# Modulation vectors of a two-layer hybrid backbone: matrix products on TensorE against weighted sums on VectorE, ScalarE and accumulating DMAs

## The chip, the cores and the metric

One NeuronCore of a Trainium2 chip runs the whole program. The metric is the device time of one execution in microseconds (us), as a median of several runs. Beside it stands one profiled execution, whose rows are quoted here: PE is TensorE, PEld its weight loads, DVE VectorE, ACT ScalarE, POOL GpSimd, SP SyncE. A "q" behind an engine's name means its sequencer, which issues transfers and waits.

## The reference

Two layers work on 512 latent and 256 context tokens of width 1024. A layer first forms modulation vectors from the two conditioning vectors `c` (for the latents) and `c_ctx` (for the context):

```python
mod_x = silu_c @ ada_w[layer] + ada_b[layer]      # [6 * 1024]
mod_c = silu_cc @ ada_w[layer] + ada_b[layer]
sh1, sc1, g1, sh2, sc2, g2 = split(mod_x, 6)      # the same for mod_c
hx = modulate(rmsnorm(x, norm1_g[layer]), sh1, sc1)
mx, mc = hybrid_mixer(hx, hc, w_in[layer], ...)   # retention and gated linear attention
x = x + g1 * (mx @ w_out[layer])
x = x + g2 * squared_relu_mlp(modulate(rmsnorm(x, norm2_g[layer]), sh2, sc2), ...)
```

`ada_w[layer]` is 1024 x 6144 float32, 24 MB for each layer. The first third (`sh1`, `sc1`) is needed before the first projection, `g1` at the output projection, `sh2`, `sc2` at the second norm, `g2` at the end of the MLP.

## The kernel before

Activations lie feature-major, 128 features by tokens. Each large product is made of three products of float32r parts (L437 to L439), so that TensorE carries nearly the whole time. The order of the work is written out by hand: `plan` is a list of items that `run` (L400) emits one after the other, and each engine executes what it was given in that order. Weights arrive as slabs of 128 x 1024 float32 (512 KB) through a ring of four `wraw` tiles; `split` (L241) casts a slab to its high part on ScalarE (L244) and subtracts on VectorE for the low part (L245). Slabs are split up to four ahead of their use, with six split slabs kept.

The attention of a layer follows `SCHEDULE` (L109): one line, here called a row and counted from 0, is one block of projections, 8 to 11 us on TensorE, and after it the stages of heads that run behind it. Stages are short: a few small products of TensorE, and chains of VectorE and ScalarE instructions. In the text, `gB` is VectorE's prefix sum of gates, `gC` ScalarE's exponentials, `qk` VectorE's products of queries and keys, `N` a head's norm.

The modulation vectors of the first layer come in two parts. The first third is made at the start, in quarters (L374, untouched). The remaining two thirds go through `ada_next` (L306): behind the block of each of the rows 0 to 15, `ada_step` loads two 512 KB pieces a step ahead and multiplies one k tile by `cs` with four products of 512 columns (L287, eight records of the profile). The second layer's vectors are made during the first layer's MLP by `ada_sums` (L324), a generator of 54 steps, one behind each MLP item: for each of six units of 1024 columns, eight steps in which VectorE adds weighted pieces to two sums (L340, L342; one for each conditioning vector), and a ninth step in which eight products of 256 columns (L348) with `onehot` add the partitions. The ninth step starts `ada_finish` (L259): ScalarE copies the row, TensorE transposes it, VectorE adds the bias.

The sums of both vectors lie in a tile that shares its place with the tables `rtab`. GpSimd squares in the MLP (L1210), multiplies in the retention stages (L983, L946), and issues a few transfers (reload L1165, spill L1250).

Of the kernel before, what the change touches and what calls it, by code (L numbers as in the profile page):

```python
# [39 lines left out]
class Item:  # L40
    """A piece of the program: emits instructions; may need weight slabs; a stage runs one block after its deps."""
# [5 lines left out]
class Chains:  # L47
    """Instruction chains that hop between engines: each tick emits the next step of every chain under way.

    Queued chains start one per tick, with at most WIDTH of them under way."""  # L50
# [45 lines left out]
class Act:  # L96
    """A moving operand in two float32r parts, made by chains for token ranges."""
# [10 lines left out]
# one block of projections and the attention stages that run behind it, per line; at most NSLOT tiles live  # L108
# [30 lines left out]
def build(ctx: ExitStack, tc, a):  # L139
# [7 lines left out]
    tp = ctx.enter_context(tc.tile_pool(name="tab", bufs=1))  # L147
    mp = ctx.enter_context(tc.tile_pool(name="mp", bufs=NSLOT))
# [23 lines left out]
    def bc(col, n):  # L172
        """[P, c] -> [P, c, n], each value repeated n times."""
        return col.rearrange("p (c o) -> p c o", o=1).to_broadcast([col.shape[0], col.shape[1], n])

    def rep(tab, c):
        """[P, n] -> [P, c, n], the row repeated c times."""
        return tab.rearrange("p (o t) -> p o t", o=1).to_broadcast([tab.shape[0], c, tab.shape[1]])
# [5 lines left out]
    # ---- constants and inputs  # L184
# [32 lines left out]
    # silu(c) of both vectors, as 32 stationary columns (30 of them zero) per k tile  # L217
# [14 lines left out]
    # ---- weight slabs: [128, 1024] and its exact split into two float32r parts  # L232
# [14 lines left out]
    class RankSlab(Slab):  # L247
        """Four copies of 32 columns per k tile: the second one's low part, the others' high parts."""
# [7 lines left out]
    # ---- adaLN vectors: mod[l][p, v, j] for feature 128 j + p  # L256
    mod = [const.tile([P, 2, 48], F32, name=f"mod{l}") for l in range(DEPTH)]

    def ada_finish(l, pt, tiles, n, fold=1):  # L259
        """pt: row 32 c + v holds, for vector v, n features from the tile tiles[c] on; `fold` such parts are summed."""  # L260
# [18 lines left out]
    def ada_step(state, l, g, kk):  # L279
        if kk == 0:  # L280
            state["pt"] = psa.tile([P, 512], F32, tag="psa", name=f"ada_{l}_{g}")
        pt = state["pt"]
        w = state.pop("w", None)
        if w is None:
            w = ada_load(l, g, kk)
        for c in range(4):
            nc.tensor.matmul(  # L287
                pt[32 * c : 32 * c + 32, :], cs[:, kk, :], w[c // 2][:, (c % 2) * 512 : (c % 2 + 1) * 512],
                start=(kk == 0), stop=(kk == KK - 1),
            )  # L290
        if kk == KK - 1:
            state["end", l, g] = ch.start(ada_finish(l, pt, [16 * g + 4 * c for c in range(4)], 512))

    def ada_load(l, g, kk):
        ws = []
        for i in range(2):
            w = wraw.tile([P, WCOL], F32, tag="raw", name=f"adaw_{l}_{g}_{kk}_{i}")
            c0 = g * 2048 + i * WCOL
            nc.sync.dma_start(w, a["ada_w"][l, kk * P : (kk + 1) * P, c0 : c0 + WCOL])
            ws.append(w)  # L300
        return ws

    ada_state = {}
    ada_queue = [(l, g, kk) for l, g in ((0, 1), (0, 2)) for kk in range(KK)]

    def ada_next():  # L306
        if ada_queue:
            l, g, kk = ada_queue.pop(0)
            ada_step(ada_state, l, g, kk)
            if ada_queue:  # L310
                ada_state["w"] = ada_load(*ada_queue[0])

    def ada_drain(l, g):
        while any(q[:2] == (l, g) for q in ada_queue):
            ada_next()
        ch.finish(ada_state["end", l, g])

    # the second layer's: weighted sums over the k tiles on the vector engine, one product to add the partitions
# [5 lines left out]
    def ada_sums(l):  # L324
        acc = tp.tile([P, 2, WCOL], F32, tag="rtab", name=f"adaacc_{l}")
        todo = [(u, kk) for u in range(6) for kk in range(KK)]
# [8 lines left out]
        for i, (u, kk) in enumerate(todo):  # L335
            w, nxt = nxt, load(i + 1) if i + 1 < len(todo) else None
            for v in range(2):
                c = cs[:, kk, v : v + 1]
                if kk == 0:
                    nc.vector.tensor_scalar(acc[:, v], w, c, None, op0=ALU.mult)  # L340
                else:
                    nc.vector.scalar_tensor_tensor(acc[:, v], w, c, acc[:, v], op0=ALU.mult, op1=ALU.add)  # L342
            yield
            if kk == KK - 1:
                pt = psa.tile([P, 512], F32, tag="psa", name=f"ada_{l}_{u}")
                for v in range(2):
                    for c in range(4):
                        nc.tensor.matmul(  # L348
                            pt[32 * c : 32 * c + 32, 0:256], onehot[:, v], acc[:, v, 256 * c : 256 * c + 256],
                            start=(v == 0), stop=(v == 1),  # L350
                        )
                ada_state["end", l] = ch.start(ada_finish(l, pt, [8 * u + 2 * c for c in range(4)], 256))
                yield

    # the first layer's shift and scale, in four quarters of 256 features each
# [18 lines left out]
    def quarter(q, middle=None, end=None):  # L374
        """Shift and scale of a quarter, even and odd k tiles apart."""
# [65 lines left out]
    def project(pt, slab, c0, acts, t0, t1, ks=None, first=0, last=None):  # L441
        """pt[:, :t1 - t0] += W[:, tile].T @ act over the k tiles `ks` of a slab part [kk, 128]."""
# [14 lines left out]
    # ---- RMSNorm over features, for a group of tokens at a time  # L457
    class Norm:
# [3 lines left out]
        def square(self, kk, t0, t1, first):  # L462
            """A chain that adds a tile's squares to the sum."""
# [14 lines left out]
        def late_square(self, kk, t0, t1):  # L478
            """A tile's squares that the product over the partitions adds to the sum."""
# [43 lines left out]
        def apply_all(self, l, shift, v, t0, t1, ks=range(KK)):  # L523
            """Chains that make the tiles `ks` of a group of tokens."""
# [15 lines left out]
    # ---- first norm, and the accumulators of the first three projections  # L540
# [63 lines left out]
    # masks and decay tables  # L604
# [6 lines left out]
    # decay of a key to its chunk's end (forward) or start (backward), per partition  # L611
    kdec = const.tile([P, nrd], F32, name="kdec")

    def setup():
# [5 lines left out]
        # log(1 - exp(ret_decay)) as log1p: ln(u) * e / (1 - u), u = 1 - e rounded  # L620
# [24 lines left out]
    def layer(l, norm):  # L645
        """The layer's items, and the norm that follows it."""
# [10 lines left out]
        def start():  # L657
# [6 lines left out]
            # retention tables per head: in-chunk weights of both directions, query decays  # L664
# [34 lines left out]
        # ---- gate ranks: low parts of the weights in rows 32 to 63, high ones elsewhere; summed by the next product  # L699
# [7 lines left out]
        # ---- gated linear attention's queries and keys, each on both partition halves  # L707
# [27 lines left out]
        def tok_blocks(nm, j0, vt, center):  # L735
            """Values token-major, one tile [token, chunk, 128] per head."""
# [36 lines left out]
        def head_out(idx, po, t0, t1, sq, o):  # L773
            """Evacuate a head's output and its square."""
# [16 lines left out]
        def gla(h):  # L791
# [16 lines left out]
            def gB():  # L808
                # 16 log gate; prefix sums per chunk, from the chunk's middle; backward ones exclusive
# [222 lines left out]
        # ---- output gates and the mixer's output  # L1032
# [47 lines left out]
        # ---- the first three projections' items  # L1080
# [354 lines left out]
```

## Time and profile before

| | us |
|---|---|
| median of 3 runs (lowest to highest) | 1659.46 (1658.64 to 1659.53) |
| the profiled execution, first to last instruction | 1658.9 |
| PE busy | 1618.7 (98%) |
| DVE busy | 946.9 (57%) |
| ACT busy | 629.5 (38%) |
| POOL busy | 201.6 (12%) |
| mean granted TensorE clock | 0.992 of full |

Busy time is a share of the whole span; a stage's limit is read from the chain of waits and from the timeline of that stage. In a timeline row the columns are start, duration, engine, line, operation, output and inputs, shapes, count, and in brackets the idle time before it with what ended it; matmuls overlap, so what one costs is read from the distance of starts.

### The profile page before, as it was taken

To read this page: it belongs to the slowest core of one execution; us is meant where nothing else is said; L and a number is where in the kernel's file an instruction comes from. 1 tells how busy PE (TensorE), PEld (TensorE's weight loads), DVE (VectorE), ACT (ScalarE), POOL (GpSimd) and SP (SyncE) were. 2 spreads that over 40 slices of the span, in tenths; PEclk is the share of its full clock that TensorE was granted. 3 is DMA by queue.
4 is the path that set the end of the run, shared out by engine and by line. 5 is a ranking of instruction groups with operands and counts; after the bars stand their busy time and mean duration, and the time that the engine had idled before them with its cause. 6 is when DMAs were issued, how large, how long until landed. Compare 5 with 4: busy or idle time off the path is not lost. (4 is left out here: it accounts for less than half of the span.)

```text
span 1658.9 us, 22890 instructions
## 1 busy us (share of the span) xinstructions
PE 1618.7 (98%) x9236; PEld 1384.2 (83%) x9236; DVE 946.9 (57%) x1491; ACT 629.5 (38%) x1083; POOL 201.6 (12%) x215
## 2 busy tenths in 40 slices
PE   5999999999999999999999999999999899999997
PEld 3778888888998888888888887888889888888887
DVE  5676664554755555555556476588466633443445
ACT  5535424562532222222212246363464532222232
POOL 3200021110111010110101121001110211010010
PEclk9999999999999999999999999999999999999999
DMA  9533433122323333333333222121123323223321
GB/s 323 175 127 126 137 108 102 39 88 90 103 89 127 115 127 109 120 102 116 126 115 127 95 88 66 51 77 52 51 89 128 103 89 102 91 100 102 102 64 51
DMA packets 57610, 173.80 MB, mean 105 GB/s; under 512 B 6208, under 2 KB 17792, under 8 KB 57504
## 3 DMA queue, kind: packets, MB, share of 16 engines
q1 hardware_dynamic: 55232, 164.85, 30.2%
q0 software_dynamic: 2272, 7.50, 1.2%
q8 instruction: 72, 1.18, 0.3%
q14 instruction: 34, 0.28, 0.0%
HBM read 168.13 MB, written 4.19 MB: 104 GB/s over the span
## 5 line engine op out<-in xcount | busy, mean ns | idle before, releaser
L437 PE MATMUL pm<-yh,hi_m 128*128 128x512 f32 (+1 forms) x800 | 279.6, 349 | 0.0
L437 PE MATMUL pm<-hidh,hi_m 128*128 128x512 f32 (+1 forms) x800 | 279.1, 349 | 0.0
L438 PE MATMUL pm<-yl,hi_m 128*128 128x512 f32 (+1 forms) x800 | 278.6, 348 | 0.0
L438 PE MATMUL pm<-hidl,hi_m 128*128 128x512 f32 (+1 forms) x800 | 278.4, 348 | 0.0
L439 PE MATMUL pm<-yh,lo_m 128*128 128x512 f32 (+1 forms) x800 | 278.2, 348 | 0.0
L439 PE MATMUL pm<-hidh,lo_m 128*128 128x512 f32 (+1 forms) x800 | 277.2, 347 | 0.0
L1208 ACT ACTIVATE relu<-pm 128x512 f32<-128x512 f32 (+1 forms) x100 | 51.1, 511 | 497.6 <-PE pm L439 493.9
L1212 DVE TENSOR_TENSOR hidl<-relu,hidh 128x512 fp32r<-128x512 f32 (+1 forms) x100 | 60.5, 607 | 296.0 <-POOL relu L1210 296.0
L1210 POOL TENSOR_TENSOR relu<-relu 128x512 f32<-128x512 f32 (+1 forms) x100 | 89.2, 893 | 760.3 <-ACT hidh L1209 760.2
L535 DVE SCALAR_TENSOR_TENSOR x<-pm,mod,x 128x512 f32<-128x512 f32 (+1 forms) x200 | 117.6, 640 | 106.6 <-PE pm L439 106.6
L437 PEld LDWEIGHTS pm<-yh,hi_m 128*128 128x128 f32 x800 | 152.6, 191 | 20.2 <-issue 1.2
L437 PEld LDWEIGHTS pm<-hidh,hi_m 128*128 128x128 f32 x800 | 151.5, 189 | 21.3 <-issue 1.1
L438 PEld LDWEIGHTS pm<-yl,hi_m 128*128 128x128 f32 x800 | 152.5, 191 | 18.8
L439 PEld LDWEIGHTS pm<-yh,lo_m 128*128 128x128 f32 x800 | 152.4, 191 | 19.0
L439 PEld LDWEIGHTS pm<-hidh,lo_m 128*128 128x128 f32 x800 | 151.1, 189 | 19.6
L438 PEld LDWEIGHTS pm<-hidl,hi_m 128*128 128x128 f32 x800 | 151.4, 189 | 18.9 <-issue 0.2
L245 DVE TENSOR_TENSOR lo_m<-raw_m,hi_m 128x1024 fp32r<-128x1024 f32 x126 | 154.0, 1222 | 10.6 <-ACT hi_m L244 10.6
L244 ACT CAST hi_m<-raw_m 128x1024 fp32r<-128x1024 f32 x128 | 129.6, 1040 | 51.6 <-DMA raw_m<-in_w_mlp 31.0
L342 DVE SCALAR_TENSOR_TENSOR adaacc<-adaw,cs,adaacc 128x1024 f32<-128x1024 f32 x84 | 103.9, 1278 | 0.0
L245 DVE TENSOR_TENSOR lo_wi<-raw_wi,hi_wi 128x1024 fp32r<-128x1024 f32 x49 | 60.6, 1249 | 29.8 <-ACT hi_wi L244 29.8
L437 PE MATMUL pwo<-yh,hi_wo 128*128 128x256 f32 (+1 forms) x224 | 70.9, 316 | 0.1
L438 PE MATMUL pwo<-yl,hi_wo 128*128 128x256 f32 (+1 forms) x224 | 70.3, 314 | 0.3 <-DVE yl L1056 0.3
(304 smaller groups left out, 2951.5 us busy)
## 6 DMA issues: line engine op xcount, KB each, us to landing
raw_m<-in_w_mlp SPq DMA_DIRECT2D x128, 512.0 KB, 3.5
adaw<-in_ada_w SPq DMA_DIRECT2D x80, 512.0 KB, 3.9
raw_wi<-in_w_in SPq DMA_DIRECT2D x58, 512.0 KB, 4.3
adaw<-in_ada_w SPq DMA_DIRECT2D x32, 256.0 KB, 6.3
raw_wo<-in_w_out SPq DMA_DIRECT2D x16, 512.0 KB, 3.4
x<-in_xT POOLq DMA_DIRECT2D x8, 384.0 KB, 7.8
x<-in_xT SPq DMA_DIRECT2D x8, 256.0 KB, 4.9
raw_wob<-in_w_out SPq DMA_DIRECT2D x4, 512.0 KB, 4.3
```

Of the source, the lines that this page charges most:

```text
L244: nc.scalar.copy(self.hi, self.raw)
L245: self.engine.tensor_sub(self.lo, self.raw, f32(self.hi))
L342: nc.vector.scalar_tensor_tensor(acc[:, v], w, c, acc[:, v], op0=ALU.mult, op1=ALU.add)
L437: nc.tensor.matmul(out, wh, xh, start=first, stop=False)
L438: nc.tensor.matmul(out, wh, xl, start=False, stop=False)
L439: nc.tensor.matmul(out, wl, xh, start=False, stop=last)
L535: nc.vector.scalar_tensor_tensor(xs[kk][:, t0:t1], pt[:, 0 : t1 - t0], mod[l][:, v, gate + kk : gate + kk + 1], xs[kk][:, t0:t1], op0=ALU. ...
L1208: nc.scalar.activation(r, pt[:, 0 : t1 - t0], AF.Relu)
L1210: nc.gpsimd.tensor_mul(r, r, r)
L1212: nc.vector.tensor_sub(a_.lo[:, t0:t1], r, f32(a_.hi[:, t0:t1]))
```

## The change

The product form of the first layer (`ada_step`, `ada_load`, `ada_queue`) goes. `ada_sums` now makes units 2 to 5 of the first layer too, in 36 steps. In each step VectorE adds the weighted piece for the latents' vector to `acc0` as before; for the context's vector ScalarE multiplies the piece in place and a transfer issued by GpSimd adds the piece to `acc1` in SBUF. The steps of the first layer are taken twice in a row of `SCHEDULE`: behind the block, and again behind the row's stages. Below, step 8a is the one behind the block of row 8, step 8b the one at the end of row 8. The sums get a pool of their own, and the scratch space for transfers that GpSimd issues is set to 2048. Comments and docstrings are blanked, lines stay in number.

```diff
+    adap = ctx.enter_context(tc.tile_pool(name="adap", bufs=1))
...
-    def ada_step(state, l, g, kk):
...
-        for c in range(4):
-            nc.tensor.matmul(
-                pt[32 * c : 32 * c + 32, :], cs[:, kk, :], w[c // 2][:, (c % 2) * 512 : (c % 2 + 1) * 512],
-                start=(kk == 0), stop=(kk == KK - 1),
-            )
...
-    ada_queue = [(l, g, kk) for l, g in ((0, 1), (0, 2)) for kk in range(KK)]
...
-    def ada_sums(l):
-        acc = tp.tile([P, 2, WCOL], F32, tag="rtab", name=f"adaacc_{l}")
-        todo = [(u, kk) for u in range(6) for kk in range(KK)]
+    def ada_sums(l, us=range(6)):
+        acc0, acc1 = acc = [adap.tile([P, WCOL], F32, tag=f"acc{v}", name=f"adaacc{v}_{l}") for v in range(2)]
+        todo = [(u, kk) for u in us for kk in range(KK)]
...
-            for v in range(2):
-                c = cs[:, kk, v : v + 1]
-                if kk == 0:
-                    nc.vector.tensor_scalar(acc[:, v], w, c, None, op0=ALU.mult)
-                else:
-                    nc.vector.scalar_tensor_tensor(acc[:, v], w, c, acc[:, v], op0=ALU.mult, op1=ALU.add)
+            c0, c1 = cs[:, kk, 0:1], cs[:, kk, 1:2]
+            if kk == 0:
+                nc.vector.tensor_scalar(acc0, w, c0, None, op0=ALU.mult)
+                nc.scalar.mul(acc1, w, c1)
+            else:
+                nc.vector.scalar_tensor_tensor(acc0, w, c0, acc0, op0=ALU.mult, op1=ALU.add)
+                nc.scalar.mul(w, w, c1)
+                nc.gpsimd.dma_start(acc1, w, accum_op=ALU.add)
             yield
...
+    def ada_next():
+        if "sums0" not in ada_state:
+            ada_state["sums0"] = ada_sums(0, range(2, 6))
+        next(ada_state["sums0"], None)
...
                 if it.slabs and l == 0:
                     plan.append(Item("ada", ada_next))
+            if l == 0:
+                plan.append(Item("ada", ada_next))
...
-                        ada_drain(0, 2)
+                        ada_drain(0, 4)
...
-            plan.append(Item("ada1", lambda: ada_drain(0, 1)))
+            plan.append(Item("ada1", lambda: ada_drain(0, 2)))
...
+                if l == 0 and u == 0 and jps == [0]:
+                    ada_drain(0, 5)
...
-    nc = _bacc.Bacc("TRN2", target_bir_lowering=False, num_devices=1)
+    nc = _bacc.Bacc("TRN2", target_bir_lowering=False, num_devices=1, dynamic_dma_scratch_size=2048)
```

## Rows read from the trace of the kernel before

**Rows 1.** The page: busy time of the engines.

```profile
PE 1618.7 (98%) x9236; PEld 1384.2 (83%) x9236; DVE 946.9 (57%) x1491; ACT 629.5 (38%) x1083; POOL 201.6 (12%) x215
```

**Rows 2.** Busy time by stretches, their sum from 50 to 482 us.

```profile
sum 432.00, PE 429.89 PEld 362.36 DVE 260.59 ACT 203.03 POOL 52.78; mean PE 11.94 PEld 10.07 DVE 7.24 ACT 5.64 POOL 1.47
```

**Rows 3.** Timeline of PE around step 1a, and around a unit's end in the MLP.

```profile
87.97 0.39 PE L439 MATMUL ps_vg<-hi_wi,hl_n 128*128 128x512 f32 x1
...
89.29 0.50 PE L437 MATMUL ps_vg<-hi_wi,hh_n 128*128 128x512 f32 x1
...
544.45 0.28 PE L439 MATMUL pm<-hidh,lo_m 128*128 128x256 f32 x1
544.65 1.07 PE L348 MATMUL ada<-adaacc,onehot 128*32 128x256 f32 x16
...
545.65 0.50 PE L437 MATMUL pm<-yh,hi_m 128*128 128x512 f32 x1
```

**Rows 4.** The page's groups: count, busy us, mean ns, idle before.

```profile
L244 ACT CAST hi_m<-raw_m 128x1024 fp32r<-128x1024 f32 x128 | 129.6, 1040 | 51.6 <-DMA raw_m<-in_w_mlp 31.0
```

**Rows 5.** DMA issues: KB each, median us to landing; then one tile's issues.

```profile
raw_m<-in_w_mlp SPq DMA_DIRECT2D x128, 512.0 KB, 3.5
...
x<-in_xT POOLq DMA_DIRECT2D x8, 384.0 KB, 7.8
...
spill<-x POOLq DMA_DIRECT2D x8, 256.0 KB, 2.5
...
L1250 POOL DMA_DIRECT2D spill<-x x8: 539/540/585, 952.0 to 969.0; - x8
```

**Rows 6.** Timelines of DVE, ACT and PE, rows 1 to 3 of the schedule.

```profile
85.22 0.95 DVE L811 TENSOR_TENSOR gl<-gl,gt 128x768 f32<-128x768 f32 x1
...
99.35 0.96 DVE L821 TENSOR_TENSOR gt<-gt,gst 128x768 f32<-128x768 f32 x1
...
101.14 2.03 ACT L244 CAST hi_wi<-raw_wi 128x1024 fp32r<-128x1024 f32 x2
...
107.95 0.94 ACT L831 ACTIVATE gt<-gt,c_sgn 128x768 f32<-128x768 f32 x1
...
104.48 0.39 PE L438 MATMUL ps_vr<-lo_wi,hh_n 128*128 128x512 f32 x1
```

**Rows 7.** The same, rows 3 and 4 of the schedule.

```profile
112.90 0.68 DVE L757 TENSOR_REDUCE vsum<-ps_vr 128x4 f32<-128x512 f32 x1
...
119.43 0.95 DVE L836 TENSOR_TENSOR gk<-gk,gl 128x768 f32<-128x768 f32 x1
...
112.50 1.06 PE L287 MATMUL ada<-adaw,cs 128*32 128x512 f32 x8
...
```

**Rows 8.** The same, row 8 of the schedule.

```profile
182.72 0.69 DVE L939 TENSOR_TENSOR rq<-ps_qa,c_sinT 64x512 f32<-64x512 f32 x1
...
180.97 1.56 PE L782 MATMUL hs<-gt,ones_v 128*128 128x512 f32 x4
182.18 0.58 PE L437 MATMUL ps_qb<-hh_n,hi_wi 128*128 128x512 f32 x1
```

**Rows 9.** The same, rows 12 and 13 of the schedule.

```profile
238.50 1.02 DVE L972 SCALAR_TENSOR_TENSOR pr<-prs,rtab 128x512 f32<-128x512 f32 x2
...
244.62 1.06 PE L287 MATMUL ada<-adaw,cs 128*32 128x512 f32 x8
```

**Rows 10.** The same, row 17 of the schedule.

```profile
303.01 0.42 DVE L1047 TENSOR_TENSOR sg<-se,ps_g 128x256 f32<-128x256 f32 x1 [0.48 <-ACT se L1046]
...
303.48 0.56 PE L437 MATMUL ps_g<-hh_n,hi_wi 128*128 128x512 f32 x1
```

**Rows 11.** Timeline of DVE in the MLP, the eighth step of a unit.

```profile
538.28 2.47 DVE L342 SCALAR_TENSOR_TENSOR adaacc<-adaw,cs,adaacc 128x1024 f32<-128x1024 f32 x2
```

**Rows 12.** PE's longest wait after the start, and the stretch around it, with PEclk.

```profile
1297.16 1.22 PE L490 MATMUL st_n<-ssum_n,ones_d 128*128 128x256 f32 x2 [4.43 <-DVE ssum_n L473]
...
1296.00:1303.00 7.00, 5.84 (x26) 5.66 (x27) 6.20 (x8) 3.48 (x9) 3.19 (x4) 0.52 0.47 151
```

More of the change, by code (lines that the diff above doesn't have):

```diff
@@ L277, in ada_finish @@
             )
-    def ada_step(state, l, g, kk):
-        if kk == 0:
[L281 to L285, printed above, removed]
-        for c in range(4):
-            nc.tensor.matmul(
-                pt[32 * c : 32 * c + 32, :], cs[:, kk, :], w[c // 2][:, (c % 2) * 512 : (c % 2 + 1) * 512],
-                start=(kk == 0), stop=(kk == KK - 1),
-            )
[L291 to L301, printed above, removed]
-    ada_state = {}
-    ada_queue = [(l, g, kk) for l, g in ((0, 1), (0, 2)) for kk in range(KK)]
[L306 to L316, printed above, removed]
+    ada_state = {}
     onehot = const.tile([P, 2, 32], F32, name="onehot")
@@ L336, in ada_sums @@
             w, nxt = nxt, load(i + 1) if i + 1 < len(todo) else None
-            for v in range(2):
-                c = cs[:, kk, v : v + 1]
-                if kk == 0:
-                    nc.vector.tensor_scalar(acc[:, v], w, c, None, op0=ALU.mult)
-                else:
-                    nc.vector.scalar_tensor_tensor(acc[:, v], w, c, acc[:, v], op0=ALU.mult, op1=ALU.add)
+            c0, c1 = cs[:, kk, 0:1], cs[:, kk, 1:2]
[6 more added lines that the diff above has]
+                nc.gpsimd.dma_start(acc1, w, accum_op=ALU.add)
             yield
@@ L348, in ada_sums, with ada_drain @@
                         nc.tensor.matmul(
-                            pt[32 * c : 32 * c + 32, 0:256], onehot[:, v], acc[:, v, 256 * c : 256 * c + 256],
+                            pt[32 * c : 32 * c + 32, 0:256], onehot[:, v], acc[v][:, 256 * c : 256 * c + 256],
                             start=(v == 0), stop=(v == 1),
                         )
-                ada_state["end", l] = ch.start(ada_finish(l, pt, [8 * u + 2 * c for c in range(4)], 256))
+                ada_state["end", l] = ada_state["end", l, u] = ch.start(
+                    ada_finish(l, pt, [8 * u + 2 * c for c in range(4)], 256)
+                )
                 yield
+    def ada_next():
+        if "sums0" not in ada_state:
+            ada_state["sums0"] = ada_sums(0, range(2, 6))
+        next(ada_state["sums0"], None)
+    def ada_drain(l, u):
+        while (l, u) not in [k[1:] for k in ada_state if k[0] == "end" and len(k) == 3]:
+            ada_next()
+        ch.finish(ada_state["end", l, u])
     QF = 256
```

## The prediction

> **What bounds the kernel.** I read the page first, then the stretches, then the timelines of the engines around each step of the modulation vectors. TensorE is busy 98% of the span [rows 1], and from 50 to 482 us, which holds the first layer's attention, it stands idle 2.1 of 432 us [rows 2]. The view of waits has no wait of TensorE between 60 and 960 us at all. So here every microsecond taken from TensorE shortens the run, and every microsecond for which TensorE must wait lengthens it. The mean busy times of VectorE (7.2 of 12 us) and ScalarE (5.6) [rows 2] suggest room, but the question is when a sum is ready, not how much is free: each engine works in the order written, so a product that is issued before its sums are there holds all of TensorE's later work.
>
> **What goes from TensorE.** Step 1a costs it 89.29 - 87.97 = 1.32 us between two products whose usual distance is 0.23 us, so 1.09 us [rows 3]. There are 16: 17.5 us. A unit of the summed form costs 545.65 - 544.45 = 1.20 us less the usual 0.12, so 1.08 us [rows 3]; four more make 4.3 us. The transposes of `ada_finish` stay the same in sum. Net: 13.1 us less. Were nothing to wait, the profiled execution would take 1658.9 - 13.1 = 1645.8 us.
>
> **What a step costs elsewhere.** VectorE: two sums take 2.47 us [rows 11], one 1.24. In the MLP it is relieved of 42 of them, which frees nothing, since TensorE waits for nothing there. In the attention it gets some 32 more. ScalarE: a product of 128 x 1024 is taken as the cast of that shape, 1.04 us [rows 4]. It must wait for VectorE's sum, as it overwrites the piece. GpSimd: 0.54 us to issue [rows 5]; it waits for ScalarE's product and for the accumulating transfer before, since both write `acc1`. Behind it stand the squares of the MLP and the retention products, rows away from their users; I cost that at nothing, and it would be a few us if a transfer took longer than a step.
>
> **How long an accumulating transfer takes** no row shows. Let L be the time from its issue to its landing. A plain 512 KB load takes 3.5 us, GpSimd's 256 KB store 2.5 us [rows 5]: about 1 us for each further 256 KB. If the sum that is read back counts like another 512 KB, L is 5.5; the stores go to DRAM and these stay in SBUF, so I take 5. The low end is 3.5, a plain load; the high end 7.8, GpSimd's 384 KB transfers in a batch [rows 5]. The Trainium skill (DMA: Bandwidth & Descriptors, Anatomy of one DMA) gives 2.0 us and the bytes over 436 GB/s, an estimate of 3.2 us for 512 KB, and (Collectives: The Full Stack, The bandwidth ceiling) says that an add inside a transfer costs by its second read, not by its arithmetic; both together give an estimate of 4.4 us, by which the time below would be some 5 us shorter. No row shows either.
>
> **Where TensorE will wait.** The ninth step of a unit, the products with `onehot`, needs the eighth step's sum, product and landing. In 9 steps a unit and two steps a row, the first layer's ninth steps fall on 4a, 8b, 13a and 17b. 4a and 13a have a block between eighth and ninth step; 8b and 17b have only a row's short stages. Times below are those of the old trace, with TensorE moved by the 1.09 us of each product that goes. The first half of the eight products needs only `acc0`, so the wait counts from 0.5 us after their start.
>
> Row 8: VectorE ends the rotary products of the block at 183.41 [rows 8]; it is behind, working without a gap, so step 7b's sum comes on top: 184.65. Step 8a: sum 185.9, product 186.9, landing 191.9 (190.4 with L 3.5; 194.7 with 7.8). TensorE has the head's norm from 180.97 to 182.18 [rows 8], less 1.09, and wants the sums at 181.6. It waits 10.3 us (8.8; 13.1; 7.6 without step 7b).
>
> Row 17: VectorE ends the gate at 303.43 [rows 10]; sum 304.7, product 305.7, landing 310.7. TensorE is through its stages at 303.48 [rows 10] and wants it at 304.0: 6.7 us (5.2; 9.5).
>
> Row 13: step 12b comes after 239.52 [rows 9]: sum 240.8, product 241.8, landing 246.8; TensorE wants it at 244.62 - 1.09 + 0.5 = 244.0 [rows 9]: 2.8 us (1.3; 5.6).
>
> Rows 1 to 4: VectorE works on three `gB` from 85.22 to 100.31 almost without a gap [rows 6]. Steps 0b and 1a put two sums ahead of them and 1b one behind: 104.0. ScalarE's product of 1b waits for that, until 105.1, and stands ahead of the evacuation of `vg2` (1.5 us) and of two casts, which took 2.03 us from 101.14 [rows 6]: the first is done at 107.7, its low part (1.2 us) at 108.9. TensorE uses that low part at 104.48 [rows 6] less 2.18, at 102.3. It waits 6.6 us. If only VectorE's three sums counted, the low part would come at 105.3: 3.0 us, the low end. From there the delay runs on. VectorE: second low part 110.1, sum of 2a 111.4. ScalarE: product 112.4, then the three `gC`, which ended at 108.89 after casts that ended at 103.17 [rows 6], 5.7 us: 118.1; product of 2b and two casts 121.4. VectorE: low part 122.6, then the evacuation of `vr0` and four products of `qk`, 112.90 to 120.38 [rows 7], with the sums of 3a and 3b: 132.6. GpSimd issues at 133.8, behind ScalarE's product and the landing of 3a, and it lands at 138.8. TensorE, 6.6 us late, wants it at 128.5 (block `vr1` from 113.5, a step behind 112.50 [rows 7], to 124.6, less 2.18): 10.3 us more. Low end, with only the two sums of row 3 behind 120.38: landing 127.4 against 124.0, 3.4 us. High end: 15.9.
>
> MLP: six ninth steps, one item of some 8 us behind the eighth. The first: sum from 538.28, alone 539.52 [rows 11]; product 540.6; landing 545.6 against 545.15 [rows 3]: 0.4 us, six times 2.7 us (0; 19.5).
>
> Waits in sum: 10.3 + 6.7 + 2.8 + 6.6 + 10.3 + 2.7 = 39.4 us; low ends 20.5, high ends 70.2.
>
> **The clock behind a wait.** After TensorE's wait of 4.43 us at 1297 the granted clock was 0.52 over 7 us [rows 12], the lower of its two levels, 1.2 GHz against 2.4: 3.4 us lost. Four of the waits are longer. The loss behind the first only makes TensorE later for 4a, so three count: 10.2 us. Low end 3.4 (8b alone), high end 17 (five).
>
> **Sum.** 1658.9 - 13.1 + 39.4 + 10.2 = 1695.4 us; the median of the runs lies 0.6 above the span, so 1696. Low ends: 1658.9 - 13.1 + 20.5 + 3.4 = 1670. High ends: 1733.
>
> **Rivals.** *TensorE isn't held*: the sums come in time and the 13.1 us stay, 1646 us. It decides at waits under 9.8 us in all (13.1 less 0.2%). For it speaks that no wait of TensorE shows today; against it, that even a landing at once leaves 186.9 - 181.6 = 5.3 us in row 8 and 1.7 in row 17, and that 3.5 us of landing alone bring row 8 to 8.8. Only if the order were not the one written would it hold. *It evens out*: waits of 10 to 16 us with no loss of clock, 1656 to 1663; that needs every low end below mine. *Transfers set the pace*: with L at 8 us or more each accumulate is still under way when the next MLP item ends, GpSimd waits for it with the squares behind it, and the ring of four pieces fills, as each is released only by a landing; SP then waits, and slabs with it. From the high ends on, 1733 us and more. *The change frees VectorE in the MLP*: 52 us of sums go, but no wait of TensorE there names VectorE, so 0 us.
>
> **How the numbers follow.** Waits as summed, 1670 to 1733: 0.80. Held up by transfers, over 1733: 0.05. Evened out: 0.05. TensorE not held: 0.10. The likeliest gives 1696; the range takes its bounds and the upper end of the evened-out case: 1661 to 1733. About 0.2% is what a measurement of this kernel can tell from no change. Faster 0.10, same 0.04, slower 0.86.
>
> **What would show it.** In the changed trace: PE busy some 13 us lower at full clock; waits of PE at L348 in rows 4, 8 and 17, ended by the accumulating transfer, 8b the longest with 4a; a wait at L438 of block `vr0` for a low part; dips of PEclk behind them; L of 4 to 6 us. Wrong would be: no wait at L348 in row 8, or an accumulate of under 3 us.

## The result, and the profile after

The changed kernel takes 1723.47 us (median of 4 runs, 1722.68 to 1725.47), the kernel before, run beside it, 1659.49 (1658.64 to 1659.65). The ratio is 1.0384, 95% interval 1.0372 to 1.0397. The profiled execution has a span of 1721.4 us, 62.5 longer than before.

The page of the changed kernel: the span, the busy time of the engines, and the granted TensorE clock in 40 slices of 43 us.

```profile
span 1721.4 us, 22991 instructions
...
PE 1623.9 (94%) x9172; PEld 1391.5 (81%) x9172; DVE 935.1 (54%) x1483; ACT 717.8 (42%) x1165; POOL 265.8 (15%) x285
...
PEclk9988889989999999999999999999999999999999
```

TensorE has 64 matmul records fewer than in [rows 1] and is yet busy 5.2 us longer. That is the clock: slices 2 to 5 and 8 (counted from 0), which lie in the attention of the first layer, stand lowest. VectorE is busy 11.8 us less, ScalarE 88.3 more, GpSimd 64.2 more. Neither of the first two is near its limit.

The first layer's attention, from the first product of `ps_vg` to the first of `pwo`, as one row for each kernel: start and end, length, busy time (and records) of PE, PEld, DVE, ACT, POOL, mean granted clock, DMA share, GB/s. First before, then after.

```profile
63.54:367.67 304.13, 304.13 (x1875) 253.24 (x1874) 181.60 (x349) 147.81 (x292) 29.73 (x29) 1.00 0.31 102
```

```profile
63.66:426.39 362.73, 309.36 (x1811) 262.59 (x1809) 219.72 (x389) 182.54 (x326) 57.10 (x57) 0.92 0.48 126
```

The stretch is 58.6 us longer. TensorE stands idle in it for 362.73 - 309.36 = 53.4 us, where it did not stand idle at all before. By the clock records it runs 61.4 us of it at 1.2 GHz instead of 2.4, and for 35.4 of these it is busy: half of that, 17.7 us, is lost. 304.1 - 13.1 + 53.4 + 17.7 = 362.1, against 362.7 measured. So nearly all of the loss lies here, and two terms carry it.

What TensorE waits for in the changed kernel: line, what ended the wait, us in total, times, longest. Rows that were there before with about the same time are left out (`st_n`, with 7.7 us against 5.7, differs most), as are two of 1.0 us or less, `ps_gk` and the second of `ps_vr`.

```profile
PE ada L314 <- DMA adaacc<-adaw: 23.2, 8, 7.4
PE ada L314 <- DVE adaacc L306: 13.1, 3, 7.3
...
PE ps_vr L415 <- ACT hi_wi L245: 8.4, 1, 8.4
...
PE pgl L780 <- ACT gq L699: 3.9, 1, 3.9
...
PE prk L948 <- ACT gq L755: 2.9, 1, 2.9
PE pds L850 <- ACT gt L838: 1.8, 1, 1.8
...
PE prk L948 <- DVE rq L917: 1.5, 1, 1.5
```

(L314 is the ninth step's product, L348 of the kernel before; L415 to L417 are its L437 to L439.) The places, on PE's timeline of the changed kernel:

```profile
108.75 0.79 PE L415 MATMUL ps_vr<-hi_wi,hh_n 128*128 128x512 f32 x1 [8.40 <-ACT hi_wi L245]
110.07 0.79 PE L416 MATMUL ps_vr<-lo_wi,hh_n 128*128 128x512 f32 x1 [0.52 <-DVE lo_wi L246]
...
135.07 0.64 PE L314 MATMUL ada<-adaacc,onehot 128*32 128x256 f32 x8 [3.53 <-DVE adaacc L306]
143.12 1.08 PE L314 MATMUL ada<-adaacc,onehot 128*32 128x256 f32 x8 [7.41 <-DMA adaacc<-adaw]
...
213.67 1.08 PE L314 MATMUL ada<-adaacc,onehot 128*32 128x256 f32 x8 [7.33 <-DVE adaacc L306]
219.72 1.08 PE L314 MATMUL ada<-adaacc,onehot 128*32 128x256 f32 x8 [4.98 <-DMA adaacc<-adaw]
```

The ninth steps stand in pairs: the first half of the products waits for VectorE's `acc0`, the second for the transfers into `acc1`. Step 4a waits 10.9 us, 8b 12.3, block `vr0` 8.9; 13a waits 2.4 and 17b 7.7.

What stands behind the wait of `vr0`, on VectorE's timeline and then on ScalarE's (here it answers to [rows 6]):

```profile
103.92 1.28 DVE L306 SCALAR_TENSOR_TENSOR adaacc<-adaw,cs,adaacc 128x1024 f32<-128x1024 f32 x1
108.79 2.36 DVE L246 TENSOR_TENSOR lo_wi<-raw_wi,hi_wi 128x1024 fp32r<-128x1024 f32 x2 [3.59 <-issue]
```

```profile
105.28 1.15 ACT L307 ACTIVATE adaw<-adaw,cs 128x1024 f32<-128x1024 f32 x1 [14.01 <-issue]
106.34 1.42 ACT L741 COPY vg<-ps_vg 128x128 f32<-128x128 f32 x8
107.59 2.06 ACT L245 CAST hi_wi<-raw_wi 128x1024 fp32r<-128x1024 f32 x2
```

ScalarE stood still for 14 us. Its next instruction was the product of step 1b, which may not overwrite the piece before VectorE has summed it, and VectorE came to that sum at 103.92, behind its prefix sums. The casts which TensorE needs stood behind the product. The profile names the cast as the releaser; the cause is two links further back. At row 8 the same happens the other way round, first ScalarE, then VectorE:

```profile
206.25 1.15 ACT L307 ACTIVATE adaw<-adaw,cs 128x1024 f32<-128x1024 f32 x1 [7.29 <-DVE adaacc L306]
207.31 1.03 ACT L245 CAST hi_wi<-raw_wi 128x1024 fp32r<-128x1024 f32 x1
```

```profile
204.94 1.28 DVE L306 SCALAR_TENSOR_TENSOR adaacc<-adaw,cs,adaacc 128x1024 f32<-128x1024 f32 x1
208.37 1.23 DVE L246 TENSOR_TENSOR lo_wi<-raw_wi,hi_wi 128x1024 fp32r<-128x1024 f32 x1 [2.15 <-ACT hi_wi L245]
...
212.33 1.28 DVE L306 SCALAR_TENSOR_TENSOR adaacc<-adaw,cs,adaacc 128x1024 f32<-128x1024 f32 x1
```

The product of 7b waits for VectorE's sum, the cast for the product, VectorE's low part for the cast (2.15 us idle), and VectorE's sum of 8a for the low part and the rotary products behind it. Two engines, busy 61% and 50% of this stretch, stand in turn for each other.

### The profile page after: what moved, and what is told of

It reads as the page before. It is cut to its first block, busy times and chain, and to the rows that moved or that the text cites. A ratio compares the mean times of both kernels' runs of the same rounds, so it can differ in the third digit from the quotient of the medians.

```text
span 1721.4 us, 22991 instructions
## 1 busy us (share of the span) xinstructions
PE 1623.9 (94%) x9172; PEld 1391.5 (81%) x9172; DVE 935.1 (54%) x1483; ACT 717.8 (42%) x1165; POOL 265.8 (15%) x285
## 5 line engine op out<-in xcount | busy, mean ns | idle before, releaser
L415 PE MATMUL pm<-yh,hi_m 128*128 128x512 f32 (+1 forms) x800 | 279.4, 349 | 0.0
L415 PE MATMUL pm<-hidh,hi_m 128*128 128x512 f32 (+1 forms) x800 | 279.1, 349 | 0.0
L417 PE MATMUL pm<-yh,lo_m 128*128 128x512 f32 (+1 forms) x800 | 278.0, 348 | 0.0
L417 PE MATMUL pm<-hidh,lo_m 128*128 128x512 f32 (+1 forms) x800 | 277.2, 347 | 0.0
L307 ACT ACTIVATE adaw<-adaw,cs 128x1024 f32<-128x1024 f32 x70 | 80.8, 1154 | 261.3 <-DVE adaacc L306 215.8
L415 PEld LDWEIGHTS pm<-yh,hi_m 128*128 128x128 f32 x800 | 152.4, 190 | 20.4 <-issue 1.2
L415 PEld LDWEIGHTS pm<-hidh,hi_m 128*128 128x128 f32 x800 | 151.4, 189 | 21.3 <-issue 1.1
L417 PEld LDWEIGHTS pm<-yh,lo_m 128*128 128x128 f32 x800 | 152.2, 190 | 18.9
L417 PEld LDWEIGHTS pm<-hidh,lo_m 128*128 128x128 f32 x800 | 151.1, 189 | 19.5
L308 POOL DMA_DIRECT2D adaacc<-adaw x70 | 61.1, 873 | 442.0 <-ACT adaw L307 418.6
L306 DVE SCALAR_TENSOR_TENSOR adaacc<-adaw,cs,adaacc 128x1024 f32<-128x1024 f32 x70 | 89.5, 1278 | 0.3
```

The lines of the kernel that those rows point to most:

```text
L306: nc.vector.scalar_tensor_tensor(acc0, w, c0, acc0, op0=ALU.mult, op1=ALU.add)
L307: nc.scalar.mul(w, w, c1)
L308: nc.gpsimd.dma_start(acc1, w, accum_op=ALU.add)
L415: nc.tensor.matmul(out, wh, xh, start=first, stop=False)
L417: nc.tensor.matmul(out, wl, xh, start=False, stop=last)
```

## The experiments

Three theories stood against each other. *Theory 1*: it is the order. A ninth step follows too closely on the chain sum, product, accumulate, and ScalarE's product holds up what is queued behind it. *Theory 2*: VectorE and ScalarE have no room for the added work in the attention; whatever is moved, the lag comes up elsewhere. *Theory 3*: it is the traffic of 70 transfers that read SBUF twice.

All runs, with the kernel before beside each group at 1660.0 to 1660.5 us. The last three columns are of the first layer's attention: length, TensorE's idle time in it, and its busy time at the lower clock.

| run | us | ratio, 95% interval | attention | idle | busy at 1.2 GHz |
|---|---|---|---|---|---|
| before | 1659.5 | | 304.1 | 0 | 0 |
| after | 1723.5 | 1.0384 [1.0372, 1.0397] | 362.7 | 53.4 | 35.4 |
| e1_gap | 1709.1 | one run | 349.3 | 39.6 | 35.3 |
| e2_layer1 | 1664.1 | 1.0023 [1.0013, 1.0033] | 303.5 | 0 | 0 |
| e3_both_dve | 1676.9 | one run | 316.7 | 21.5 | 6.6 |
| e4_pool_add | 1728.8 | one run | 372.8 | 61.4 | 39.0 |
| e5_once | 1716.8 | 1.0341 [1.0325, 1.0356] | 303.5 | 10.2 | 9.8 |
| e6_place | 1702.2 | 1.0256 [1.0241, 1.0271] | 341.9 | 33.8 | 31.4 |
| e7_place_dve | 1681.3 | 1.0129 [1.0112, 1.0145] | 324.7 | 26.1 | 13.9 |
| e8_own_tile | 1726.1 | one run | 365.6 | 57.8 | 34.4 |
| e8b2_two_products | 1693.5 | one run | 336.2 | 35.5 | 21.2 |
| e9_half | 1669.2 | 1.0054 [1.0037, 1.0071] | 313.6 | 12.7 | 4.4 |
| e10_two_products_place | 1670.7 | 1.0059 [1.0042, 1.0076] | 314.6 | 18.1 | 9.6 |
| e11_further_apart | 1659.0 | 0.9995 [0.9986, 1.0004] | 301.4 | 10.5 | 1.4 |

**Which layer, and which half of a step.** The kernel before with the second layer's change alone (sums by VectorE, products and accumulates, `ada_step` kept):

> The kernel before with the second layer's sums alone changed (ScalarE products and accumulating transfers in the MLP; the first layer keeps its products on TensorE). Theory 1: only the six ninth steps of the MLP wait, 3.0 us in sum in the changed kernel; 1662 to 1664 us. Theory 2: the same. Theory 3, traffic of 42 transfers of 512 KB beside the slabs: TensorE or ScalarE waits for slabs in the MLP, 1668 us or more. That relief of VectorE in the MLP pays: below 1658.

It came at the upper end of what theories 1 and 2 named: 3.7 us slower, and TensorE's only new row of waits is 2.6 us in all, three times at most 0.9, for landings at the ninth steps of the MLP. The 42 transfers as such cost little there. The changed kernel with both sums of the first layer on VectorE, without products and transfers in the attention:

```diff
+            if l == 0:
+                for t, c in ((acc0, c0), (acc1, c1)):
+                    ...  # as L340, L342 of the kernel before
+            elif kk == 0:
```

> The changed kernel with both sums of the first layer on VectorE (no ScalarE product, no accumulating transfer in the attention; the second layer stays as changed). Theory 1, the chain of sum, product and landing behind an in-order queue: in row 8 the wait is two more sums instead of product and landing, 6.8 us instead of 12.3, in row 17 about 2 instead of 7.7, in row 4 about 2 instead of 10.9, before vr0 still about 7; about 1675 us. Theory 2, load: VectorE gets 32 sums of 1.24 us more, so 1723 or above. Theory 3, traffic: all of the loss in the attention goes, about 1650.

That came too, though VectorE has 32 sums more to do. The 46.6 us by which the changed kernel is slower than this one hang on ScalarE's products and the accumulates in the attention. What stays is 8.2 us ahead of `vr0`, where VectorE alone is late, and 6.8 us at 8b, as expected.

**Traffic.** GpSimd adds the product itself, and no transfer accumulates:

```diff
-                nc.gpsimd.dma_start(acc1, w, accum_op=ALU.add)
+                nc.gpsimd.tensor_add(acc1, acc1, w)
```

> The changed kernel with each accumulating transfer replaced by an addition on GpSimd (128 x 1024, some 2.5 us by its lo_wi subtraction), in both layers. Theory 1: a chain 2.5 us shorter at each ninth step and no wait in the MLP; the chain of sum and product behind VectorE stays; 1705 to 1714. Theory 2: 1723. Theory 3, traffic of 36 MB of transfers: 1680 or below.

It became slower, not faster (theory 2 had named 1723): the loss is there without accumulating transfers. But this run brings a cost of its own, and so tells less than was hoped. The groups from 60 to 370 us, operation, count, busy us and mean ns; the changed kernel first, then this one:

```profile
L246 DVE TENSOR_TENSOR lo_wi<-raw_wi,hi_wi 128x1024 fp32r<-128x1024 f32 x21 | 25.5, 1224 | 38.1 <-ACT hi_wi L245 32.3 <-issue 5.8
L306 DVE SCALAR_TENSOR_TENSOR adaacc<-adaw,cs,adaacc 128x1024 f32<-128x1024 f32 x28 | 35.8, 1280 | 0.3
L791 DVE TENSOR_TENSOR_SCAN gt<-seg,gl 128x768 f32<-128x768 uint8 x4 | 7.0, 1758 | 0.1
```

```profile
L308 POOL TENSOR_TENSOR adaacc<-adaacc,adaw 128x1024 f32<-128x1024 f32 x28 | 72.4, 2586 | 187.6 <-ACT adaw L307 182.7 <-ACT gest L803 4.8
L246 DVE TENSOR_TENSOR lo_wi<-raw_wi,hi_wi 128x1024 fp32r<-128x1024 f32 x20 | 40.0, 2016 | 32.1 <-ACT hi_wi L245 26.2 <-issue 5.8
L306 DVE SCALAR_TENSOR_TENSOR adaacc<-adaw,cs,adaacc 128x1024 f32<-128x1024 f32 x28 | 39.5, 1411 | 0.3
L791 DVE TENSOR_TENSOR_SCAN gt<-seg,gl 128x768 f32<-128x768 uint8 x4 | 9.1, 2278 | 0.1
```

VectorE's subtraction takes 2.02 us in place of 1.22 beside GpSimd's adds, and everything that waits for low parts moves back with it. The Trainium skill (SBUF — State Buffer, Who interferes with whom) says that a VectorE instruction with two inputs in SBUF contends with a GpSimd instruction that reads SBUF. These rows agree, the weighted sum (1.28 to 1.41 us) much less than the subtraction; what makes that difference isn't known from these runs.

**An empty step ahead of the ninth.** The distance from the eighth step to the ninth doubles, the ninth steps fall on 4b, 9b, 14b, 19b:

```diff
             if kk == KK - 1:
+                if l == 0:
+                    yield
                 pt = psa.tile(...)
```

> The changed kernel with one empty step between the eighth and the ninth step of a unit of the first layer, so that a block of projections always lies between the last sum and the products that need it (ninth steps at 4b, 9b, 14b, 19b). Theory 1, the place of the ninth step: the waits at L314 of rows 8 and 17 (12.3 and 7.7 us) and of row 13 (2.4) go, with the half clock behind two of them; of the 10.9 us in row 4 some 4 go; about 1693 us. Theory 2, load: VectorE and ScalarE have too much to do in the attention wherever the products stand; the waits move to other lines, within 8 us of 1723. Theory 3, traffic: accumulating transfers hold up the loads; no change, 1723.

The waits at L314 fell from 36.3 to 7.5 us, as theory 1 wants, but the total only by 14.4, to a time between the two forecasts. In row 9 TensorE now waits 4.6 us for ScalarE's copy of rotated queries (ahead of `pkt`), in others 3.4 us for a gate (`hs`) and 3.4 for `pgl`; `vr0` keeps its 8.4. The clock loses as much as before. This is the lag of which theory 2 speaks, or the part of theory 1 that isn't about the ninth step.

**The places.** One step a row, the other twelve behind the items of the output projection and the first of the MLP:

> The changed kernel with one step a row in the attention of the first layer (behind the block, as the products stood before); the twelve steps that are left stand behind items of the output projection (8) and the first MLP items (4). Theory 1: a block lies between all steps, no sum stands ahead of row 1's backlog for ScalarE to wait on; waits at L314 of under 3 us in the attention, 1 to 2 us before vr0, 3 us in the MLP; about 1651 us. Theory 2, load: the work is the same, only spread over a longer stretch; 1680 to 1700. Theory 3, traffic: the transfers are as many; 1700 or more.

The attention came out much as expected: 303.5 us long, 10.2 idle, no wait at L314, though `vr0` waits 3.3 us and not 1 to 2. The loss moved to where the twelve steps were put. GpSimd's timeline there, then PE's:

```profile
378.31 4.09 POOL L1143 DMA_DIRECT2D x<-in_xT  x7
384.03 0.54 POOL L1143 DMA_DIRECT2D x<-in_xT  x1 [1.62 <-DMA adaacc<-adaw]
385.83 0.90 POOL L308 DMA_DIRECT2D adaacc<-adaw  x1 [1.26 <-ACT adaw L307]
398.97 0.89 POOL L308 DMA_DIRECT2D adaacc<-adaw  x1 [12.24 <-DMA adaacc<-adaw]
```

```profile
392.63 1.08 PE L314 MATMUL ada<-adaacc,onehot 128*32 128x256 f32 x8 [13.19 <-DVE adaacc L306]
404.80 1.08 PE L314 MATMUL ada<-adaacc,onehot 128*32 128x256 f32 x8 [11.10 <-DMA adaacc<-adaw]
```

The accumulate of 385.83, behind eight reloads of 384 KB from the same engine, landed at 398.42: 12.6 us, where the median is 4.9. VectorE's sum ahead of the first of the two waits had to wait for its piece, which SP issued at 383.53 and which landed only at 391.19, 7.7 us later, where the median of such loads is 4.5. The expectation had left both out: a miss, and in this one place the transfers do set the pace. They don't at the other pair of waits, 18.7 us at 500 and 506: 13.7 of it are for VectorE's sum, which began at 498.98, behind the work of the second norm.

So the steps stay in the attention, from row 3 on (behind the tight rows 0 to 2), with ninth steps only behind a block, at 7a, 12a, 17a and 22a:

```diff
-                if it.slabs and l == 0:
+                if it.slabs and l == 0 and r >= 3:
...
-            if l == 0:
+            if l == 0 and r >= 3 and r not in (11, 16, 21):
```

> The changed kernel with its 36 steps of the first layer moved only: none in rows 0 to 2 (VectorE's three gB), then two a row, and every ninth step behind a block (7a, 12a, 17a, 22a), with a whole row between eighth and ninth step for three of the four units. Number and kind of instructions and transfers are those of the change. Theory 1, place: no wait before vr0, none of over 3 us at L314 in the attention; the 13.1 us come back less a few for ScalarE standing behind VectorE, and the MLP keeps its 4 us; 1650 to 1665. Theory 2, load of VectorE and ScalarE: the same work in fewer rows, 1700 or more. Theory 3, traffic: 1700 or more.

A miss again: `vr0` waits 1.0 us in place of 8.9, the ninth steps 13.8 in all, but waits of 1 to 4 us appear ahead of eight other tiles (`pgl` 3.8, `ps_ka` 2.6, `pkt` 2.4, `psb` 2.3 among them), and TensorE is busy for 31 us at the lower clock. The same places with both sums of both layers on VectorE:

> The same places, with both sums of both layers on VectorE (no ScalarE product, no accumulating transfer; the second layer as in the kernel before). Theory 1: no product before a sum, none behind a transfer; nearly all of the 13.1 us stay, 1646 to 1653. Theory 2, load of VectorE (72 sums of 1.24 us in rows 3 to 21): 1665 or more.

A miss as well, though 21 us better than with products. Its largest wait is in row 22, 9.4 us for ScalarE's copy of the finished row, which stands behind the gates. After these two runs theory 2 looked the stronger.

**ScalarE's product in a tile of its own.** The product no longer overwrites the piece, so it need not wait for VectorE's sum:

```diff
-                nc.scalar.mul(w, w, c1)
-                nc.gpsimd.dma_start(acc1, w, accum_op=ALU.add)
+                pr = adap.tile([P, WCOL], F32, tag="prod", name=...)
+                nc.scalar.mul(pr, w, c1)
+                nc.gpsimd.dma_start(acc1, pr, accum_op=ALU.add)
```

> The changed kernel with ScalarE's product written to a tile of its own (one buffer) instead of over the piece, so that it no longer waits for VectorE's sum of the same step. Theory 1, ScalarE in its order behind VectorE: the wait before vr0 falls from 8.9 to about 3, row 4 from 10.9 to about 6, row 8 from 12.3 to about 6, row 17 from 7.7 to about 6, and the waits for ScalarE at pgl and prk (9.2 in sum) mostly go; 1682 to 1698. Theory 2 and 3: within 8 us of 1723.

With one such tile nothing was won. ScalarE's timeline tells why:

```profile
126.89 1.15 ACT L308 ACTIVATE adapr<-adaw,cs 128x1024 f32<-128x1024 f32 x1 [5.60 <-issue]
135.05 1.15 ACT L308 ACTIVATE adapr<-adaw,cs 128x1024 f32<-128x1024 f32 x1 [7.01 <-DMA adaacc<-adapr]
```

It waits for no sum now, but for the landing of the accumulate before, which still reads the tile. One wait had taken the place of the other. The run also shows that giving the piece's own place back sooner, which this form does too, is worth nothing by itself. With two tiles (`bufs=2`):

> After, with ScalarE's product written into one of two tiles of its own instead of over the piece, so that it need not wait for VectorE's sum of the same piece, and need not wait for the landing of the accumulate just before it, only for the one before that. If ScalarE standing behind VectorE is what costs (theory 1), the wait ahead of vr0 is 6 us or less, the ninth steps of rows 4 and 8 wait no longer than in the changed kernel (10.9 and 12.3 us), no product waits for its own tile, and the total is 1695 to 1712 us. If the load on VectorE and ScalarE together is what costs (theory 2), the waits only change places and the total stays at 1715 to 1727 us.

This is the run that decides. 1693.5 us, 1.5 below the range of theory 1 and 30 less than the changed kernel, with the same work on VectorE (935.9 us busy against 935.1) and ScalarE (714.0 against 717.8). It is one run, but 30 us are far more than the runs of any kernel here lie apart (at most 6.3). ScalarE's timeline ahead of `vr0`, to be held against the one of the changed kernel:

```profile
99.37 2.03 ACT L245 CAST hi_wi<-raw_wi 128x1024 fp32r<-128x1024 f32 x2
101.98 1.15 ACT L308 ACTIVATE adapr<-adaw,cs 128x1024 f32<-128x1024 f32 x1 [0.58 <-ACT hi_wi L245]
```

The casts are done at 101.4, six microseconds before they began in the changed kernel; what `vr0` still waits for (5.8 us) is VectorE. Of TensorE's waits in the list of the changed kernel these are left:

```profile
PE ada L315 <- DMA adaacc<-adapr: 22.3, 4, 7.3
...
PE ada L315 <- DVE adaacc L306: 7.4, 3, 5.3
PE ps_vr L417 <- DVE lo_wi L246: 5.8, 1, 5.8
```

All waits at `pgl`, `pds` and `prk` are gone, those of the MLP too. Row 4 still waits 8.2 us, row 8 12.6 (0.3 more than before), row 13 2.4, row 17 6.6. ScalarE's products still waited three times, 8.4 us in sum, for an accumulate that read their tile. GpSimd's timeline at row 8:

```profile
194.29 0.86 POOL L309 DMA_DIRECT2D adaacc<-adapr  x1 [4.63 <-DMA adaacc<-adapr]
202.12 0.86 POOL L309 DMA_DIRECT2D adaacc<-adapr  x1 [6.96 <-DMA adaacc<-adapr]
```

Each accumulate waits for the landing of the one before, 7.8 us from issue to issue: two steps within a row run into each other here.

**Both together.** Two product tiles, and the places of e6_place:

> Two products of ScalarE in tiles of their own, as in the run before, and the places of the run on places: steps of the first layer from row 3 on, ninth steps behind the blocks of rows 7, 12, 17 and 22. With the order of products as in the run on places alone the time was 1702 us, with the tiles alone 1694 us. Theory 1: in the run with the tiles alone the waits of TensorE in the attention were 5.8 us ahead of vr0, 8.2 in row 4, 12.6 in row 8, 2.4 in row 13 and 6.6 in row 17, 35.6 in sum; the places take all of these away but some 4 to 8 us at row 7 and row 22, and the clock stays up: 1646 to 1657 us, below the kernel before. Theory 2, the load of VectorE and ScalarE: waits of some 30 us come up again in other rows as they did with the places alone, and the total is 1680 us or more.

The total missed the range of theory 1 by 14 us, and that of theory 2 by 9. Of the eight waits that e6_place showed, 0.7 us at `pkt`, 1.1 at a gate and 0.3 to 0.4 at three others are left. What is left besides is the ninth steps themselves: 8.1 us in row 7, whose eighth step lies only one block ahead (6b), 1.3 in row 12, and 5.0 in row 22. In the next run the ninth steps stand at 8a, 13a, 18a and 23a, the eighth at 6b, 12a, 17a and 22a. That moves only the first ninth step further from its eighth; the expectation says it of each, but the other three pairs go one row down together, at the distance that they had. The edit, against the run before:

```diff
-                if it.slabs and l == 0 and r >= 3:
+                if it.slabs and l == 0 and r >= 3 and r != 7:
...
-            if l == 0 and r >= 3 and r not in (11, 16, 21):
+            if l == 0 and r >= 3 and r not in (7, 12, 17, 22):
```

> As the run before (two products of ScalarE in tiles of their own, steps from row 3 on), but with each ninth step a step further from its eighth: ninth steps at 8a, 13a, 18a and at the end of row 23, the eighth at 6b, 12a, 17a and 22a. The run before waited 8.1 us in row 7, 1.3 in row 12, 5.0 in row 22 (3.2 for the landing, 1.8 for the copy of the row behind ScalarE's gates) and some 3 us elsewhere. Theory 1, the distance from the eighth step's product to the ninth step: these 14 us go, and with them the dips of the clock behind them; 3 to 5 us of waits stay against 13.1 us of products that are gone: 1649 to 1658 us, below the kernel before. Theory 2, the load: VectorE stays a row behind in rows 16 to 22, the waits come up at other lines, and the total is 1665 us or more.

1659.0 us, a ratio of 0.9995 with an interval that holds 1: the whole loss is undone, though it is no gain that can be measured. The range of theory 1 was missed by 1 us. The 8.1 us of row 7 are gone, as its eighth step is now further ahead, and the 1.3 of row 12 with them; the last unit, no further apart than before, waits 7.9 us in row 23 where it waited 5.0 in row 22. The attention, and what TensorE still waits for at its end:

```profile
63.53:364.96 301.43, 290.94 (x1810) 252.32 (x1809) 224.51 (x390) 183.96 (x332) 61.51 (x61) 0.99 0.60 155
```

```profile
363.05 1.08 PE L315 MATMUL ada<-adaacc,onehot 128*32 128x256 f32 x8 [7.87 <-DMA adaacc<-adapr]
```

VectorE and ScalarE are busy in this stretch for 224.5 and 184.0 us, more than in the changed kernel (219.7 and 182.5), and TensorE idles 10.5 us instead of 53.4. With that theory 2 falls as far as room is meant: the room was there. What the coupled engines lacked was freedom to run apart. Theory 3 falls with it: all 70 accumulating transfers are still there. The last wait is one accumulate behind another, with the reloads issued right behind it:

```profile
350.07 0.85 POOL L309 DMA_DIRECT2D adaacc<-adapr  x1 [4.24 <-DMA adaacc<-adapr]
356.87 0.85 POOL L309 DMA_DIRECT2D adaacc<-adapr  x1 [5.95 <-DMA adaacc<-adapr]
357.48 4.04 POOL L1146 DMA_DIRECT2D x<-in_xT  x7
```

By the ledger of idle and clock, most of the 13.1 us would show without it; that is an estimate and wasn't tried.

**Half of the change with the old tools.** The kernel before, with units 4 and 5 as products in rows 0 to 7, and units 2 and 3 as sums of both vectors on VectorE, one step a row from row 5 to 22 (ninth steps at 13a and 22a):

> The kernel before, with half of the change and none of its tools: the second layer as it was; of the first layer's four units, the last two stay products on TensorE (rows 0 to 7), the other two are made as sums of both vectors on VectorE, one step behind the block of each row from row 5 to row 22, the ninth steps on 13a and 22a with a block ahead of them. TensorE loses 8 products (8.7 us) and gains two ninth steps (2.2 us). If each row has room for one step of 2.5 us on VectorE, nothing waits and the total is 1653 to 1657 us, below the kernel before. If VectorE and ScalarE have no room (theory 2), the lag shows as waits in rows 13 to 22 and the total is 1660 us or more.

Slower by 0.5%, the time that theory 2 named: 12.7 us idle and 2.2 lost to the clock against 6.5 saved. But 7.2 us of it are one wait in row 22, again for ScalarE's copy of the row behind the gates; no other wait is longer than 1.6 us. Row 22 was a bad place for a ninth step in e6_place, e7_place_dve and e10_two_products_place too.

## Why the prediction was right, and where its sizes were off

The forecast was 1696 us; it came to 1723.5, within the range. The direction and the mechanism held, and four terms of the sum can be compared with their measured values. That the range held the time is partly luck: its upper end was made in large part of transfers of 7.8 us, with 19.5 us of waits in the MLP, and neither came. What came instead, 11.1 us of other waits and four more dips of the clock, stood in no term of the sum.

**What goes from TensorE**: 13.1 us. With it the ledger of the attention closes to within 1.5 us in every run that makes all four units there in the summed form: in e8b2_two_products 304.1 - 13.1 + 35.5 + 10.6 = 337.1 against 336.2, in e11_further_apart 304.1 - 13.1 + 10.5 + 0.7 = 302.2 against 301.4.

**The landing L**, taken as 5 us, was right. Of the changed kernel, DMA issues, KB each, median us to landing:

```profile
adaacc<-adaw POOLq DMA_DIRECT2D x70, 512.0 KB, 5.0
```

They land in 4.5 to 7.1 us (in the kernels with two product tiles the median is 5.5). The estimates from the Trainium skill (DMA: Bandwidth & Descriptors, Anatomy of one DMA), 3.2 us, and with the second read 4.4, lie below every one of the 70. The issue on GpSimd, taken as 0.54 us from [rows 5], is 0.87; ScalarE's product, taken as 1.04 from [rows 4], is 1.15.

**The waits named** were 39.4 us in the sum and 45.2 in the trace:

| place | predicted | measured |
|---|---|---|
| `vr0` | 6.6 | 8.9 |
| 4a | 10.3 | 10.9 |
| 8b | 10.3 | 12.3 |
| 13a | 2.8 | 2.4 |
| 17b | 6.7 | 7.7 |
| MLP, six | 2.7 | 3.0 |

All but one lie between their bounds; `vr0` lies above the 6.6 us that were also its high end. The waits at L314 are ended by the transfer (23.2 us) as foretold, but for 13.1 us by VectorE's own sum. At `vr0` the chain was the one told: sum of 1b, product, casts; the product ended at 106.4, where the prediction had 105.1, and TensorE stood at the block from 100.4 on. At 4a the wait fits although its two ends don't: the transfer landed at 143.1 and not at 138.8, and TensorE came 3.5 us later too, so the small difference is luck. The working has slips there: 128.5 comes out only with three products off 124.6 (1a to 3a), not with the 2.18 that stand beside it; by that rule the low end's 124.0 would be 124.8, and the casts' 121.4 adds up to 121.2. None moves the sum by more than 1 us. At 8b the landing came 4.5 us behind its issue, but VectorE's sum was late, as the step 7b's product had held ScalarE's cast and the cast VectorE.

**The step that failed is what lies between the ninth steps.** The prediction wrote that ScalarE's product must wait for VectorE's sum, and worked it out for rows 1 to 4 alone; for the other rows it counted a step as so much busy time. There the waits at `pgl` and `ps_gk` (4.8 us), `prk` (4.5) and `pds` (1.8) came up, 11.1 us in no term. e8b2_two_products shows the cause: free the product from the sum, and all of them go.

**The clock** was put at 10.2 us, three dips of 3.4; it took 17.7. The dips are seven in the attention. Stretches of the changed kernel around the three longest (columns as above; the granted clock is the third number from the end):

```profile
104.00:115.00 11.00, 5.73 (x13) 4.16 (x14) 5.16 (x8) 6.90 (x15) 1.72 (x2) 0.54 0.58 151
135.00:150.00 15.00, 7.52 (x64) 5.68 (x66) 5.14 (x19) 3.34 (x6) 0.86 (x1) 0.54 0.45 116
...
210.00:225.00 15.00, 6.35 (x27) 3.79 (x28) 7.84 (x12) 6.23 (x9) 0.86 (x1) 0.54 0.69 168
```

Around waits of 8.4, 10.9 and 12.3 us the granted clock is 0.54 over 11 to 15 us, against 0.52 over 7 us at the 4.43 us of [rows 12]. These dips are longer than that one, but TensorE stands idle in about half of each, and idle time loses nothing. By half of its busy time at the lower clock the seven dips cost 1.7 to 3.1 us each, and the dip of [rows 12] by the same measure 2.8, not 3.4. So the size was put a little high, and the number far too low. The prediction left out the dip behind the first wait, since it would only make TensorE later for 4a; but 4a waited as long as predicted and the loss of the first came on top. Two more dips stand at waits that it didn't have (`pgl`, `prk`). A small wait could be followed by one as well: 3.4 us behind 13a's 2.4; in e8b2_two_products the same wait had none.

Sum: 1658.9 - 13.1 + 45.2 + 11.1 + 17.7 = 1719.8, of a span of 1721.4; the 1.6 us left weren't traced (`st_n`, outside the attention, waits 2.0 us longer than before).

**The rivals.** *TensorE isn't held* fell as predicted, by the arithmetic of row 8. e11_further_apart shows what it needed: another order and a tile that the change doesn't have. *It evens out* fell: waits of 8 to 12 us came with the clock's loss, here and in e8_own_tile and e8b2_two_products. *Transfers set the pace* didn't decide: without accumulates the time was 1728.8, and with all of them, in e11_further_apart, 1659.0. It holds in one place that the change doesn't use, beside the reloads. *The change frees VectorE in the MLP* was rightly put at 0: e2_layer1 relieves VectorE of 48 sums (the prediction counted 42), some 50 us (896.7 busy against 946.9), and is slower by 3.7.

## What to carry to other kernels

When work is moved from a busy engine to two idle ones, count the waits between the two first: an in-place product that must come after its neighbour's sum makes two in-order engines into one, and here a pair of tiles for the product gave back 30 us of 64. Then see how far each result lies ahead of its user in the written order: with the pair of tiles, other places gave another 23 us, and more distance for one unit, with the rest a row later, the last 12. The pair alone left 34 us, other places alone 42; the last places without the pair weren't tried. A sum of the waits is a low estimate when stretches of lower clock come with them: here 53 us of waits brought 18 more.

## What the runs showed of the hardware

An accumulating transfer of 512 KB within SBUF took 5.0 us in the median, one issued behind eight loads of 384 KB 12.6. Its issue stood 0.87 us on GpSimd's timeline, a plain load's of 384 KB 0.54. In a stretch with 28 adds on GpSimd, VectorE's subtraction of 128 x 1024 went from 1.22 to 2.02 us, its scan of 128 x 768 from 1.76 to 2.28, while the weighted sum went only from 1.28 to 1.41.
